# The context's modulation columns: from row products on DVE to float32 matmuls, started four steps sooner

## The chip, the core and the metric

One core of a Trainium2 chip runs the whole program in a single launch. The metric is the device time of one execution in microseconds (us). The kernel before took 3189.59 us, the median of three runs (3187.55 to 3194.36).

## The reference, cut to what matters

The program is a two-layer block (attention and a large product-key expert layer) on 256 tokens of width 1024, followed by a second block with recurrent mixers and a mixture of experts. The second block starts its recurrent states from a context of 256 rows. The context is normalised and modulated, and the modulation is what the change touches:

```
def _modulation(cvec, w, b, n):
    m = jax.nn.silu(cvec) @ w[:, : n * D_MODEL] + b[: n * D_MODEL]
    return jnp.split(m, n, axis=-1)
...
cm = _modulation(c_ctx, w_mod[i], b_mod[i], 2 if last else 6)
hc = _rmsnorm(ctx, norm_mix_pre[i]) * (1.0 + cm[1]) + cm[0]
sf_c = _state_features(hc, w_in[i], gdn_conv[i], gdn_a_log[i], gdn_dt_bias[i])
```

There is one layer here, so `n` is 2. A vector of 1024 values goes through SiLU and is multiplied by a 1024 x 2048 float32 weight, 8 MB. None of it depends on the first block's tokens. It can be worked out at any time before the context's features are needed.

## The kernel before, in words

Activations stand transposed: features on the 128 partitions, tokens along the free dimension. A weight tile is 128 x 1024 float32, 512 KB, loaded by a DMA from SP's queue. For the large projections `slot` splits it into a rounded high part on ACT (L281) and a remainder on DVE or POOL (L285), and each product takes three matmuls of these halves (`mm3`). The first four remainders of a phase go to POOL.

The opening runs two strands at once. The main strand is the first block: `ln_in` loads x, normalises it and transposes it on TensorE into h; `attention` projects keys, queries and values, rotates keys and queries (`rope`), splits them (`qsplit`, `ksplit`) and goes on to the scores. The side strand is the generator `context1` (L1234): the modulation, the context's normalisation, its features (`gdn_feat`) and its retention states. `tick(n)` runs the side strand n steps further, where a step is the work up to the next `yield`. So the places of the `tick` calls, with the numbers in `STEPS`, set the program order of the two strands. The scheduler that fills each engine's queue goes by a priority that follows the program order, with side instructions set back by `lag`, 100 places in the first layer, and by when it expects an instruction's inputs and buffers to be ready. Each engine then works through its queue in order.

The side strand has 20 steps. In the kernel before, two run at the end of `ln_in`, three after the key's split, four after the first query pair's rotation, four after the second's, three after the value projection, then two after each of two further query pairs.

The modulation in the kernel before: the vector c_ctx is loaded as one row broadcast to 128 partitions (`silu_row`, L947) and passed through SiLU. The weight lies with output columns on the partitions, so one tile of 128 outputs x 1024 inputs gives 128 modulation values: DVE multiplies the tile by the row and sums along the free dimension (L1247). Sixteen tiles make the 16 columns of `mctx`. The tiles take turns in the side strand's staging buffers rawB, whiB and wloB, two of each, which the context's projections use later. The first step only allocates; eight steps do two tiles each; the next two do the context's normalisation and transposes.

PSUM is handed out by `ps`: main work takes psA, side work psB, two buffers each.

Of the kernel before, what the change touches and what calls it, by code (L numbers as in the profile page):

```python
# [17 lines left out]
AF = mybir.ActivationFunctionType  # L18
OP = mybir.AluOpType
# [3 lines left out]
P = 128  # L23
D = 1024
S = 256
NT = 2
NC = 8
L = 2
# [102 lines left out]
def _colspec():  # L131
    s = [("lnin_g", 8), ("lnin_b", 8)]
    for l in range(L):
        s += [(f"ln1_g{l}", 8), (f"ln1_b{l}", 8), (f"ln2_g{l}", 8), (f"ln2_b{l}", 8), (f"gn{l}", 8), (f"qn{l}", 1), (f"kn{l}", 1)]
    s += [("mixpre", 8), ("ffnpre", 8), ("mixpost", 8), ("ffnpost", 8), ("bmod", 48), ("conv", 36), ("retgn", 4), ("gdnw", 4)]
    return s


# [4 lines left out]
def _pack(a):  # L143
    f = np.float32
    A = {k: np.asarray(v) for k, v in a.items()}
    out = _consts()
    col = lambda v: np.ascontiguousarray(v.reshape(-1, P).T)
    dup = lambda v: np.concatenate([v, v])[:, None]
    cols = {"lnin_g": col(A["ln_in_g"]), "lnin_b": col(A["ln_in_b"])}
    for l in range(L):  # L150
        cols[f"ln1_g{l}"], cols[f"ln1_b{l}"] = col(A["ln1_g"][l]), col(A["ln1_b"][l])
        cols[f"ln2_g{l}"], cols[f"ln2_b{l}"] = col(A["ln2_g"][l]), col(A["ln2_b"][l])
        cols[f"gn{l}"] = col(np.concatenate([A["gn_a_g"][l], A["gn_b_g"][l]]))
        cols[f"qn{l}"], cols[f"kn{l}"] = dup(A["qn_g"][l]), dup(A["kn_g"][l])
    cols["mixpre"], cols["ffnpre"] = col(A["norm_mix_pre_2"][0]), col(A["norm_ffn_pre_2"][0])
    cols["mixpost"], cols["ffnpost"] = col(A["norm_mix_post_2"][0]), col(A["norm_ffn_post_2"][0])
    cols["bmod"] = col(A["b_mod_2"][0])
    cv = A["gdn_conv_2"][0]
    cols["conv"] = np.concatenate([col(cv[k]) for k in range(3)], 1)
    cols["retgn"], cols["gdnw"] = col(A["ret_gn_w_2"][0]), col(A["gdn_norm_w_2"][0])  # L160
    out["cols"] = np.ascontiguousarray(np.concatenate([cols[n] for n, _ in COLSPEC], 1))
    rows = {"sink0": A["sink"][0], "sink1": A["sink"][1], "rdecay": A["ret_log_decay_2"][0].reshape(-1),
            "alog": A["gdn_a_log_2"][0].reshape(-1), "dtb": A["gdn_dt_bias_2"][0].reshape(-1), "rbias": A["router_bias_2"][0]}
    out["rows"] = np.ascontiguousarray(np.concatenate([rows[n] for n, _ in ROWSPEC])[None])
    out["brows"] = np.ascontiguousarray(np.stack([A["ln2_g"][L - 1], A["ln2_b"][L - 1], A["c_2"][0], A["c_ctx_2"]]))

    def tslots(w):
        k, n = w.shape
        return np.ascontiguousarray(w.reshape(k // P, P, n // P, P).transpose(2, 1, 0, 3)).reshape(n // P, P, -1)

    def kslots(w):
        k, n = w.shape
        return np.ascontiguousarray(w.reshape(k // 512, 4, P, n // 256, 256).transpose(3, 0, 2, 1, 4)).reshape(n // 256, k // 512, P, -1)

    hd = lambda b, h: np.arange(b + h * 64, b + h * 64 + 64)
    perm = [np.arange(512, 640), np.arange(1280, 1408)]
    perm += [np.concatenate([hd(0, t), hd(0, t + 4)]) for t in range(4)]
    perm += [np.concatenate([hd(768, t), hd(768, t + 4)]) for t in range(4)]
    perm = np.concatenate(perm)
    permv = np.concatenate([np.arange(640, 768), np.arange(1408, 1536)])  # L180
    out["win"] = np.stack([tslots(A["w_in"][l][:, perm]) for l in range(L)])
    out["winv"] = np.stack([kslots(A["w_in"][l][:, permv])[0] for l in range(L)])
    out["wo"] = np.stack([kslots(A["w_o"][l]) for l in range(L)])
    out["wq"] = np.stack([tslots(A["peer_wq"][l]) for l in range(L)])
    out["keys"] = np.ascontiguousarray(A["peer_keys"].transpose(0, 4, 1, 2, 3)).reshape(L, P, 2, 1024)
    u = A["peer_u"].reshape(L, 128, 128, 8, 128)
    out["u"] = np.ascontiguousarray(u.transpose(0, 2, 4, 3, 1)).reshape(L, 128, P, 1024)
    out["v"] = A["peer_v"].reshape(L, 128, 128, 1024)
    out["x"] = A["x"][0]
    out["ctx"] = A["ctx_2"][0]  # L190
    out["wmod"] = np.ascontiguousarray(A["w_mod_2"][0].T).reshape(48, P, D)
    w = A["w_in_2"][0]
    out["wrkv"] = kslots(w[:, 0:1024])
    out["wt2"] = tslots(np.concatenate([w[:, 0:512], w[:, 1024:2048], w[:, 2064:]], 1))
    out["wgab"] = np.ascontiguousarray(w[:, 2048:2064].reshape(NC, P, 16).transpose(1, 0, 2)).reshape(P, -1)
    t4 = lambda m: np.ascontiguousarray(m.reshape(4, P, 4, 2, P).transpose(2, 1, 3, 0, 4)).reshape(4, P, -1)
    out["wro"] = t4(A["w_ret_out_2"][0])
    out["wgo"] = t4(A["w_gdn_out_2"][0])
    out["wo2"] = kslots(A["w_o_2"][0])
    out["wr"] = np.ascontiguousarray(A["w_router_2"][0].reshape(NC, P, NE).transpose(1, 0, 2)).reshape(P, -1)  # L200
    gu = lambda g, u: np.concatenate([g, u], -1).reshape(-1, 4, 2, P, 512).transpose(0, 1, 3, 2, 4).reshape(-1, 4, P, 1024)
    out["moegu"] = np.concatenate([gu(A["w_sh_gate_2"][None], A["w_sh_up_2"][None]), gu(A["w_gate_2"][0], A["w_up_2"][0])])
    out["moed"] = np.concatenate([A["w_sh_down_2"].reshape(1, 2, P, 1024), A["w_down_2"][0].reshape(NE, 2, P, 1024)])
    return {k: np.ascontiguousarray(v, f) for k, v in out.items()}
# [4 lines left out]

STEPS = ((3, 4, 3, 2, 0, 1), (2, 1, 3, 2, 0, 3))
GSTEPS = (1, 0, 1, 2, 0, 1, 1, 0, 2, 0, 2, 1, 1, 1, 0, 0, 0, 2, 0, 0, 0, 0, 0, 2)


class K:
# [262 lines left out]
    def ln_in(self, a):  # L479
        nc = self.nc  # L480
        with self.tc.tile_pool(name="lnin", bufs=1) as pool:
            ys = []
            for t in range(2):
                ys.append(self.t(pool, [D], "lny", bufs=2))
                nc.sync.dma_start(ys[t], self.I["x"][t * P:(t + 1) * P, :])
            self.load_consts()
            for t, y in enumerate(ys):
                z = self.normalize(pool, [y[:, 0:512], y[:, 512:]], t)
                self.to_T(z, a, self.col["lnin_g"], self.col["lnin_b"], t)
            self.tick(2)  # L490
# [47 lines left out]
    def attention(self, l, a):  # L538
        nc, I = self.nc, self.I
        with ExitStack() as es:  # L540
# [61 lines left out]
            self.ksplit(KK[:, 0], KL[:, 0], ksb)  # L602
            self.tick(STEPS[l][0])
            qrope(0, qg0)
            self.tick(STEPS[l][1])
            qsum(1, sq1)
# [627 lines left out]
    def context1(self, es):  # L1234

        nc, I, tc = self.nc, self.I, self.tc
        cp = es.enter_context(tc.tile_pool(name="c1", bufs=1, side="right"))
        a = self.act(cp, NC, "hc", False)
        yield
        with tc.tile_pool(name="cm", bufs=1, side="right") as mp:  # L1240
            cb = self.t(mp, [D], "cb")
            self.silu_row(cb, 3)
            for j in range(16):
                pr = self.t(self.st, [D], ("rawB", "whiB", "wloB")[j % 3], bufs=2)
                nc.sync.dma_start(pr, I["wmod"][j])
                eng = nc.vector
                eng.scalar_tensor_tensor(pr, pr, 1.0, cb, op0=OP.mult, op1=OP.mult, accum_out=self.mctx[:, j:j + 1])  # L1247
                if j % 2:
                    yield
            nc.vector.tensor_tensor(self.mctx, self.mctx, self.col["bmod"][:, 0:16], op=OP.add)  # L1250
            g = self.scale_col(mp, self.col["mixpre"], self.mctx[:, 8:16], "cg")
            for t in range(NT):
                y = self.t(mp, [D], "cty", bufs=2)
                nc.sync.dma_start(y, I["ctx"][t * P:(t + 1) * P, :])
                self.to_T(self.rms_z(mp, y), a, g, self.mctx[:, 0:8], t, mp)
                yield
        self.dbg("hcT", a.hi.bitcast(F32).rearrange("p a n -> p (a n)"))
        fp = es.enter_context(tc.tile_pool(name="c2", bufs=1, side="right"))
        cs = self.t(fp, [self.CS], "cs")
        yield from self.gdn_feat(self.feat_views(cs), a, fp)  # L1260
        nc.sync.dma_start(self.dfeat, cs)
        rS = self.t(fp, [2, 512], "rS")
        yield from self.ret_states(fp, a, rS)
        nc.sync.dma_start(self.dret, rS.rearrange("p d n -> p (d n)"))
# [732 lines left out]
```

## Time and profile before

| | us |
|---|---|
| median of three runs | 3189.59 |
| lowest and highest | 3187.55, 3194.36 |
| profiled execution, its own time | 3194.2 |
| span in the profile, first to last instruction | 3192.4 |
| PE busy | 3017.8 |
| DVE busy | 2460.4 |
| ACT busy | 1636.2 |

PE is TensorE, PEld its weight loads, DVE VectorE, ACT ScalarE, POOL GpSimd, SP the engine that issues most DMAs. A line such as L1247 is one of the kernel file; names such as whiB are tiles, with buffer numbers left out. The granted clock is the share of full speed that TensorE's throttle gave; matmul ends are modelled, so PE can look busy while it is not at its peak.

### The profile page before, as it was taken

Reading aid. Unit: us, or ns where it says so; the run is one execution under the profiler, and the core shown is the slowest. Engines: PE = TensorE matmul, PEld = TensorE weight load, DVE = VectorE, ACT = ScalarE, POOL = GpSimd, SP = SyncE. Lnnn points to the kernel's source line nnn. Section 1 sums busy time; section 2 is a strip of 40 time slices with the busy share of each in tenths; the row PEclk is TensorE's granted clock in tenths of the full one; section 3 lists DMA queues with packets and bytes.
Section 4 is the critical chain, followed back from the end, with each engine's and each line's share of the span. In section 5 each row is a group of like instructions: output and inputs, shape, how many; then the busy total and the mean of one; then the engine's idle time right before and its main releaser. Section 6 shows DMA issues by size and latency. Waiting matters only on the chain. (4 is left out here: it accounts for less than half of the span.)

```text
span 3192.4 us, 51605 instructions
## 1 busy us (share of the span) xinstructions
PE 3017.8 (95%) x19882; PEld 2710.4 (85%) x19882; DVE 2460.4 (77%) x4140; ACT 1636.2 (51%) x2298; POOL 517.0 (16%) x311
## 2 busy tenths in 40 slices
PE   5999999999999799999999999978998999999997
PEld 5889999998888688999999888878997787777776
DVE  7555998876677776699887767767777888888886
ACT  4554444454544434444445454443344677766675
POOL 2010220000000423122000000012323222222221
PEclk8899999999999899999999999989998999999999
DMA  6335555567788312555556778842232887787875
GB/s 250 104 103 172 172 177 199 194 216 245 235 264 277 123 40 80 179 179 175 199 196 221 249 229 275 264 154 73 93 126 97 286 304 278 285 288 277 293 281 187
DMA packets 181199, 641.80 MB, mean 201 GB/s; under 512 B 20816, under 2 KB 21328, under 8 KB 180304
## 3 DMA queue, kind: packets, MB, share of 16 engines
q1 hardware_dynamic: 175824, 621.64, 57.0%
q0 software_dynamic: 5120, 16.78, 1.3%
q8 instruction: 158, 2.59, 0.3%
q14 instruction: 97, 0.79, 0.1%
HBM read 617.87 MB, written 20.46 MB: 200 GB/s over the span
## 5 line engine op out<-in xcount | busy, mean ns | idle before, releaser
L281 ACT CAST whiB<-rawB 128x1024 fp32r<-128x1024 f32 x433 | 454.1, 1049 | 446.0 <-PE psB L254 171.8
L281 ACT CAST whiA<-rawA 128x1024 fp32r<-128x1024 f32 x423 | 443.5, 1049 | 406.6 <-PE psA L254 159.4
L285 DVE TENSOR_TENSOR wloA<-rawA,whiA 128x1024 fp32r<-128x1024 f32 x390 | 515.1, 1321 | 154.9 <-ACT whiA L281 148.3
L285 DVE TENSOR_TENSOR wloB<-rawB,whiB 128x1024 fp32r<-128x1024 f32 x405 | 507.2, 1252 | 126.7 <-ACT whiB L281 121.9
L285 POOL TENSOR_TENSOR xlo<-xraw,xhi 128x1024 fp32r<-128x1024 f32 x64 | 170.1, 2658 | 520.6 <-ACT xhi L281 510.5
L254 PE MATMUL psA<-hh,whiA 128*128 128x256 f32 x840 | 244.7, 291 | 6.2 <-ACT hh L294 5.7
L254 PE MATMUL psA<-hh,wloA 128*128 128x256 f32 x840 | 243.4, 290 | 7.5 <-POOL wloA L285 6.5
L254 PE MATMUL psA<-hl,whiA 128*128 128x256 f32 x840 | 243.2, 290 | 2.9 <-DVE hl L295 2.9
L254 PE MATMUL psB<-hh,wloB 128*128 128x256 f32 x832 | 238.4, 287 | 4.8 <-DVE wloB L285 4.8
L254 PE MATMUL psB<-hh,whiB 128*128 128x256 f32 x832 | 239.6, 288 | 0.1
L254 PE MATMUL psB<-hl,whiB 128*128 128x256 f32 x832 | 237.7, 286 | 0.0
L254 PE MATMUL acc<-whiA,hh 128*128 128x512 f32 x512 | 199.2, 389 | 0.0
L254 PE MATMUL acc<-wloA,hh 128*128 128x512 f32 x512 | 199.2, 389 | 0.0
L254 PE MATMUL acc<-whiB,hh 128*128 128x512 f32 x512 | 199.2, 389 | 0.0
L254 PE MATMUL acc<-wloB,hh 128*128 128x512 f32 x512 | 199.2, 389 | 0.0
L254 PE MATMUL acc<-whiA,hl 128*128 128x512 f32 x512 | 199.2, 389 | 0.0
L254 PE MATMUL acc<-whiB,hl 128*128 128x512 f32 x512 | 199.2, 389 | 0.0
L285 POOL TENSOR_TENSOR wloB<-rawB,whiB 128x1024 fp32r<-128x1024 f32 x28 | 74.5, 2662 | 739.7 <-ACT whiB L281 739.7
L285 POOL TENSOR_TENSOR wloA<-rawA,whiA 128x1024 fp32r<-128x1024 f32 x33 | 87.3, 2650 | 628.1 <-DVE zlnry L363 348.2
L254 PEld LDWEIGHTS psA<-hh,wloA 128*128 128x128 f32 x840 | 165.3, 197 | 9.0 <-POOL wloA L285 7.3
L254 PEld LDWEIGHTS psA<-hh,whiA 128*128 128x128 f32 x840 | 165.1, 197 | 7.2 <-ACT hh L294 6.5
L254 PEld LDWEIGHTS psA<-hl,whiA 128*128 128x128 f32 x840 | 165.0, 196 | 3.9 <-POOL wloA L285 1.9
(842 smaller groups left out, 8660.6 us busy)
## 6 DMA issues: line engine op xcount, KB each, us to landing
rawA<-in_moegu SPq DMA_DIRECT2D x130, 512.0 KB, 4.7
rawB<-in_moegu SPq DMA_DIRECT2D x130, 512.0 KB, 5.2
rawA<-in_u SPq DMA_DIRECT2D x128, 512.0 KB, 3.4
rawB<-in_u SPq DMA_DIRECT2D x128, 512.0 KB, 3.3
rawA<-in_v SPq DMA_DIRECT2D x128, 512.0 KB, 4.5
rawB<-in_v SPq DMA_DIRECT2D x128, 512.0 KB, 4.5
xraw<-in_moed SPq DMA_DIRECT2D x128, 512.0 KB, 5.9
rawB<-in_wt SPq DMA_DIRECT2D x40, 512.0 KB, 3.2
```

The costliest lines, as they stand in the source:

```text
L254: self.pe = self.nc.tensor.matmul(out, lhsT, rhs, start=start, stop=stop, skip_group_check=True).ins
L281: self.nc.scalar.copy(hi[:, :n], w[:, :n])
L285: i = (eng or self.nc.vector).tensor_tensor(lo[:, :n], w[:, :n], hi[:, :n].bitcast(F32), op=OP.subtract)
```

## The change

The weight of the two modulation vectors is laid out a second time as `wmodc`, with inputs on the partitions, in the tile form of the other projections. The vector c_ctx becomes eight columns of the constants tile (`cctx`) and leaves the rows that are broadcast. A SiLU runs over 128 x 8 values. For each of eight steps n, two tiles are loaded; each tile is eight 128 x 128 weights that stand in the array while one column of the vector moves through, accumulating over the eight input chunks into one PSUM column. DVE adds the bias while it reads the two columns out of PSUM. Arithmetic is plain float32.

A `tick(4)` is put into `ln_in` ahead of the normalisation, and `STEPS` for the first layer is lowered by one at its first three entries, of which the second is used twice.

```diff
-    s += [("mixpre", 8), ("ffnpre", 8), ("mixpost", 8), ("ffnpost", 8), ("bmod", 48), ("conv", 36), ("retgn", 4), ("gdnw", 4)]
+    s += [("mixpre", 8), ("ffnpre", 8), ("mixpost", 8), ("ffnpost", 8), ("bmod", 48), ("cctx", 8), ("conv", 36), ("retgn", 4), ("gdnw", 4)]
...
+    cols["cctx"] = col(A["c_ctx_2"])
...
+    out["wmodc"] = tslots(A["w_mod_2"][0][:, 0:2 * D])
...
-STEPS = ((3, 4, 3, 2, 0, 1), (2, 1, 3, 2, 0, 3))
+STEPS = ((2, 3, 2, 2, 0, 1), (2, 1, 3, 2, 0, 3))
...
             self.load_consts()
+            self.tick(4)
             for t, y in enumerate(ys):
...
-            cb = self.t(mp, [D], "cb")
-            self.silu_row(cb, 3)
-            for j in range(16):
-                pr = self.t(self.st, [D], ("rawB", "whiB", "wloB")[j % 3], bufs=2)
-                nc.sync.dma_start(pr, I["wmod"][j])
-                eng = nc.vector
-                eng.scalar_tensor_tensor(pr, pr, 1.0, cb, op0=OP.mult, op1=OP.mult, accum_out=self.mctx[:, j:j + 1])
-                if j % 2:
-                    yield
-            nc.vector.tensor_tensor(self.mctx, self.mctx, self.col["bmod"][:, 0:16], op=OP.add)
+            cc = self.t(mp, [8], "cc")
+            nc.scalar.activation(cc, self.col["cctx"], AF.Silu)
+            for n in range(8):
+                ps = self.ps()
+                for z in range(2):
+                    w = self.t(self.st, [D], ("rawB", "whiB", "wloB")[(2 * n + z) % 3], bufs=2)
+                    nc.sync.dma_start(w, I["wmodc"][2 * n + z])
+                    for c in range(NC):
+                        self.mm(ps[:, z:z + 1], w[:, c * P:(c + 1) * P], cc[:, c:c + 1], z + c == 0, z == 1 and c == NC - 1)
+                nc.vector.tensor_tensor(self.mctx[:, 2 * n:2 * n + 2], ps[:, 0:2], self.col["bmod"][:, 2 * n:2 * n + 2], op=OP.add)
+                yield
```

## Rows read from the trace of the kernel before

**Rows 1.** The page, part 1: PE's busy time, share of span, instructions.

```profile
PE 3017.8 (95%) x19882; PEld 2710.4 (85%) x19882; DVE 2460.4 (77%) x4140; ACT 1636.2 (51%) x2298; POOL 517.0 (16%) x311
```

**Rows 2.** Opening by stretch: length, busy time by engine, granted clock, DMA share, GB/s.

```profile
0.00:22.00 22.00, 4.61 (x17) 3.29 (x17) 13.06 (x43) 11.82 (x18) 7.09 (x10) 1.00 0.79 274
22.00:49.00 27.00, 23.77 (x156) 22.74 (x155) 20.80 (x38) 7.31 (x12) 11.09 (x8) 0.94 0.83 311
49.00:64.40 15.40, 5.77 (x24) 2.84 (x23) 13.41 (x35) 9.28 (x20) 3.71 (x3) 0.73 0.38 154
64.40:100.00 35.60, 33.27 (x249) 32.62 (x250) 27.54 (x61) 23.58 (x37) 0.00 (x0) 0.88 0.56 179
100.00:140.00 40.00, 32.28 (x209) 28.61 (x208) 20.78 (x45) 19.56 (x37) 0.00 (x0) 0.79 0.24 80
140.00:230.00 90.00, 89.69 (x699) 81.74 (x698) 53.89 (x157) 43.44 (x101) 7.60 (x5) 1.00 0.27 94
```

**Rows 3.** Timeline of PE: start, us, instruction, [idle before <-releaser].

```profile
21.59 0.58 PE L254 MATMUL psA<-hh,whiA 128*128 128x256 f32 x1 [2.00 <-ACT hh L294]
...
64.39 0.58 PE L254 MATMUL psA<-whiA,hh 128*128 128x256 f32 x1 [8.13 <-ACT whiA L281]
67.08 1.97 PE L262 MATMUL psB<-cst,rmsz 128*128 128x128 f32 x8 [2.10 <-DVE rmsz L970]
...
106.09 0.55 PE L254 MATMUL psA<-KK,Q 128*128 128x256 f32 x1 [2.18 <-DVE Q L527]
...
133.60 1.97 PE L262 MATMUL psB<-cst,gvT 128*128 128x128 f32 x8 [4.68 <-ACT gvT L994]
```

**Rows 4.** Line 1247's row products: count, min/median/max ns, first and last start.

```profile
L1247 DVE SCALAR_TENSOR_TENSOR rawB<-rawB,cb x6: 1219/1225/1411, 16.1 to 62.2; 128x1024 f32<-128x1024 f32 x6
L1247 DVE DVE_READ_ACCUMULATOR rawB<-rawB,cb x6: 77/81/83, 17.4 to 63.3; 128x1 f32 x6
L1247 DVE SCALAR_TENSOR_TENSOR whiB<-whiB,cb x5: 1209/1221/3309, 18.7 to 50.5; 128x1024 f32<-128x1024 f32 x5
...
L1247 DVE SCALAR_TENSOR_TENSOR wloB<-wloB,cb x5: 1211/1218/1226, 21.1 to 52.0; 128x1024 f32<-128x1024 f32 x5
```

**Rows 5.** Timeline of ACT, POOL and DVE near the start.

```profile
10.64 1.03 ACT L281 CAST whiA<-rawA 128x1024 fp32r<-128x1024 f32 x1
...
11.75 4.65 POOL L285 TENSOR_TENSOR wloA<-rawA,whiA 128x1024 fp32r<-128x1024 f32 x2 [11.32 <-ACT whiA L281]
...
14.99 1.06 ACT L950 ACTIVATE cb<-cb 128x1024 f32<-128x1024 f32 x1
...
16.07 1.41 DVE L1247 SCALAR_TENSOR_TENSOR rawB<-rawB,cb 128x1024 f32<-128x1024 f32 x1 [1.96 <-ACT cb L950]
```

**Rows 6.** Timeline of SP's queue.

```profile
3.06 0.91 SPq L266 DMA_DIRECT2D rawA<-in_win  x2
```

**Rows 7.** DMA issues of the opening: size of one, median us to landing.

```profile
rawA<-in_win SPq DMA_DIRECT2D x6, 512.0 KB, 3.8
...
cb<-in_brows SPq DMA_DIRECT2D x1, 512.0 KB, 8.6
```

**Rows 8.** Timeline of PE: float32 matmuls in a row, merged.

```profile
100.36 1.91 PE L254 MATMUL psB<-cst,ssq 128*128 128x1 f32 x16
...
109.03 3.78 PE L254 MATMUL psB<-cst,zgkry 128*128 128x128 f32 x16 [0.86 <-DVE zgkry L363]
```

**Rows 9.** Two shorter stretches, columns as in rows 2.

```profile
64.40:73.00 8.60, 6.50 (x29) 6.21 (x30) 8.60 (x26) 4.80 (x8) 0.00 (x0) 0.50 0.75 237
...
106.00:114.00 8.00, 7.05 (x27) 6.00 (x28) 4.33 (x10) 3.58 (x9) 0.00 (x0) 0.50 0.31 112
```

**Rows 10.** Timelines of ACT and DVE ahead of the value projection.

```profile
56.27 1.66 ACT L535 CAST KK<-ksb 64x256 fp32r<-64x256 f32 x4 [4.79 <-DVE ksb L505]
...
63.30 1.99 ACT L281 CAST whiA<-rawA 128x1024 fp32r<-128x1024 f32 x2
63.47 0.16 DVE L1250 TENSOR_TENSOR mctx<-mctx,cols 128x16 f32<-128x16 f32 x1
```

More of the change, by code (lines that the diff above doesn't have):

```diff
@@ L164, in _pack @@
     out["rows"] = np.ascontiguousarray(np.concatenate([rows[n] for n, _ in ROWSPEC])[None])
-    out["brows"] = np.ascontiguousarray(np.stack([A["ln2_g"][L - 1], A["ln2_b"][L - 1], A["c_2"][0], A["c_ctx_2"]]))
+    out["brows"] = np.ascontiguousarray(np.stack([A["ln2_g"][L - 1], A["ln2_b"][L - 1], A["c_2"][0]]))
     def tslots(w):
```

## The prediction

> **What bounds the kernel now.** The page's first part comes first: TensorE is busy for 3017.8 of 3192.4 us [rows 1]. Most of the program is a stream of matmuls with almost no gaps, so only gaps, or matmuls at the half clock, can be won. The change touches the context's side work alone, so I next cut the opening into stretches [rows 2]. From 140 us on PE is busy for 89.69 of 90 us. Before that it isn't: 4.61 of the first 22 us, 23.77 of the 27 us from 22 to 49, 5.77 of the 15.4 us from 49 to 64.4, 33.27 of 35.6 and 32.28 of 40 us after it. In those stretches the granted clock is 0.94, 0.73, 0.88 and 0.79, a mix of the full 2.4 GHz and half of it. Whatever this change is worth is decided between 10 and 140 us; later work starts sooner or later by the same amount.
>
> What ends PE's waits there? At the start the normalised input: the first projection matmul starts at 21.59, after ACT and DVE have turned h into its two halves. Then one wait of 8.13 us before the V projection at 64.39, for ACT's cast whiA; 2.10 us for the context's rmsz; 2.18 us for a Q half; 4.68 us for the context's gvT [rows 3]. The two engines named were not free for the main path: DVE is busy for 20.80 of the 27 us and 13.41 of the 15.4 us [rows 2], and the row products of the changed lines are the large optional share of that.
>
> **What goes.** Sixteen row products on DVE: medians 1.225, 1.221 and 1.218 us, and one of 3.31, beside a POOL subtraction; each is followed by an accumulator read of 0.08 [rows 4]. With their means that is 6 x 1.267 + 5 x 1.637 + 5 x 1.220 = 21.9 us, and 16 x 0.08 = 1.3: 23.2 us of DVE. The SiLU over 1024 columns (1.06 us on ACT) goes, and so does its 512 KB broadcast load, which took 8.6 us to land [rows 5, 7]. An 8-column SiLU takes their place. Its ACT table load stays, likely earlier; its cost has the old 1.06 us as upper end and zero as the lower. I take zero, as the work is a hundredth.
>
> **What comes.** 128 float32 matmuls of one column. The nearest row is the same form: 16 float32 matmuls of 128x1 in 1.91 us, 0.119 each. At the half clock the nearest row is 16 float32 matmuls, 128x128, in 3.78 us, 0.236 each, in a stretch whose granted clock is 0.50 [rows 8, 9]. So 128 cost 15.2 us at the full clock (taken, since PE now has work between the projections) and 30.2 us at the other end; below 15 nothing excludes a little, as single ends are modelled. Eight small additions on DVE replace one of 0.16 us [rows 10] (between the main path's operations, 1.1 us more); one addition ends each group and frees its PSUM buffer, two of which alternate. The queue of PE is in order: behind a modulation matmul that waits for its 512 KB tile stand the transposes of h and the projections, and ACT and DVE wait for those.
>
> **What moves.** Four steps are put ahead of the normalisation. The first only opens; the next three issue six weight tiles on SP, 48 matmuls and three additions. Now the first two win tiles go out on SP at 3.06 us [rows 6], and every modulation tile later. In program order the six tiles now come early; a side step's priority is set back by 100 places, and by my count of the instructions between them they still precede win. So the main loads pass behind 6 x 512 KB. At the 311 GB/s of the stretch from 22 to 49 [rows 2] one tile takes 1.69 us, six 10.1. Four later places take one step fewer each, until the counts meet at the V projection (16 steps before and after), so nothing after that is moved in program order, and the queues of POOL and ACT get the same work behind it.
>
> **The sum, stretch by stretch** (against the profiled execution: span 3192.4, its own time 3194.2, while the three timed runs have a median of 3189.59).
>
> 1. To the first projection. ACT loses 1.06 us and DVE two row products (1.41 and, by the median, 1.22) that stand between hr and hl now [rows 4, 5], so h is ready about 3.7 us sooner if nothing else were late. Next late is the weight: win lands near 3.06 + 3.8 [rows 6, 7] + 10.1 = 17 us, its cast takes 1.03 and POOL's subtraction 4.65 for two [rows 5]: about 20.3 for the first, 22.7 for the second, where the second is needed one tile of matmuls later. That leaves 1.5 of the 3.7 us: **-1.5** (ends -3.7 and +1, the latter if the transposes stand behind six tiles that land one per 1.69 us).
> 2. 22 to 49. By 22 us the DMA engines moved 22 x 274 GB/s = 6.0 MB, at a busy share of 0.79; with cb gone and the holes filled that is room for about eight modulation tiles beside x, constants and win. The other eight, 64 matmuls, add 64 x 0.119 = 7.6 us to PE. The stretch has 27 - 23.77 = 3.2 us free, and 0.06 x 27 = 1.6 us is what its lower clock costs at most. **+3** (ends: -4.8, all tiles before 22 and both losses gone; +12, all sixteen in it with only the 3.2 us filled).
> 3. 49 to 64.4. Three row products (two here at 1.3 with their reads, and one at 62.20) leave DVE's chain: 3.9 us. The key's rotation, which now queues with the queries' because its small steps wait between row products, can move ahead of it, about 3 us more by my reading. The cover that remains is ACT's order: KK at 56.27, the Q casts, the rmsz squares, whiB, and only then whiA at 63.30 [rows 10]. **-6** (ends: 0, if whiA still comes last after the same work; -8.1, the whole wait).
> 4. After 64.4. The modulation ends near 49 instead of 63.5, so the context's rmsz wait of 2.10 us is gone or filled: **-2** (ends 0 and -9, if the waits of 2.18 and 4.68 go too).
>
> -1.5 + 3 - 6 - 2 = **-6.5 us**: 3187.7 in the profiled execution's terms, **3183.1** beside the median of the timed runs.
>
> Weighing the clock: the rows say that PE stands at the half clock after its longest wait, 0.50 from 64.4 to 73 us, while its matmuls follow each other [rows 9]. The Trainium skill, in "TensorE: Matmul & The Clock Gate", section "HAM oscillation — how this bites in real kernels", states that bursts of matmuls shorter than the wait for the next DMA keep the clock throttled; read so, it speaks against this change and is the third rival below; the trace of before has no such bursts to show it.
>
> **Rivals.**
> - *Larger gain.* The context's features come so early that PE's later waits (2.18 and 4.68, and some half-clock time in 100 to 140) are filled as well: -6.5 - 7.5 = -14, **3176**. For it: the granted clock of 0.79 there [rows 2] shows how much lies open. Against: those waits are chains within the features, whoever starts first.
> - *The wait stays.* whiA still stands last in ACT's order, the side work fills that time as before, and PE has only the added matmuls: -1.5 + 3 = +1.5, **3191**. For it: side and main work stands ahead of whiA in that order now [rows 10].
> - *Half clock.* A tile's eight matmuls take 0.95 us, its transfer 1.69, so PE works in short bursts and the 64 matmuls after 22 us cost 0.236: 64 x 0.117 = 7.5 more: +1, **3190.5**. Against: between bursts there are projections.
> - *Slower: PE becomes the bound.* Most modulation matmuls fall into 22 to 49, where PE is 88% busy. Fifteen or sixteen tiles there cost 15.2 - 3.2 = +12; with -6 and -1.5 from steps 3 and 1, and step 4 paid by a later start (+2), that is +6.5 to +7, **3196.5**. It decides once what comes after 22 us exceeds 3.2 + 1.5 + 6 = 10.7 us, 90 matmuls or 11 tiles. For it: main loads wait behind six tiles. Against: PE has 17 free us before 22.
>
> **Chances.** Forecast 0.50 (own range 3178 to 3188), larger gain 0.15, wait stays 0.13, half clock 0.07, slower 0.15. A difference of 0.2% (6.4 us) is about what measurement tells from none. Half of the forecast's chance is beyond it, all of the larger gain, and 0.02 of the spread of the next two: faster 0.42. Same: 0.25 of the forecast, 0.14 of these two, 0.02 of the last: 0.41. Slower: 0.13 and 0.04 of their upper ends: 0.17. Range: from 3173, below the larger gain, to 3198, just over the slower case, leaves out the tails of both, and the joint ends of the four steps (-25.6 and +13).
>
> **What would show it.** Right: no row product on DVE; groups of float32 128x1 matmuls on PE from about 10 us, near 0.12 us each; the last addition of the columns before 52 us; the V projection's first matmul near 60 instead of 64.39; and PE's stream at 140 us some 6 us ahead. Step 1 is wrong if the first projection matmul starts after 23 us with PE waiting for a modulation tile or for win; step 2 if the sixth weight tile of the projections ends much after 50; step 3 if a wait of 8 us before V is still there. The forecast falls as a whole if the lead at 64 us is lost by 140 us to waits inside the context's features.

## The result and the profile after

The changed kernel takes a median of 3230.65 us (3222.45 to 3233.53), the kernel before 3190.62 us beside it: a ratio of 1.0119, interval 1.0105 to 1.0132. It is 40 us slower. The forecast was 3183.1, the range ended at 3198.

The page of the changed kernel, its span and the first line of part 1, which answers to [rows 1]:

```profile
span 3230.4 us, 52091 instructions
PE 3069.6 (95%) x20138; PEld 2764.5 (86%) x20138; DVE 2444.3 (76%) x4115; ACT 1634.8 (51%) x2297; POOL 511.2 (16%) x311
```

Against the profiled execution of before (span 3192.4) the span grew by 38.0 us. TensorE's busy time grew by 51.8 us (3069.6 - 3017.8), its idle time fell by 13.8 us (174.6 to 160.8). So TensorE didn't come to wait more; it came to work longer. And it has 256 more instructions (20138 - 19882), where 128 matmuls were added: each float32 matmul leaves two records (a record is one entry of the profile).

The opening of the changed kernel by stretch, in the columns of [rows 2] (length, busy time of PE, PEld, DVE, ACT, POOL, granted clock, DMA share, GB/s):

```profile
0.00:22.00 22.00, 11.20 (x54) 11.23 (x54) 8.67 (x36) 5.94 (x10) 0.19 (x4) 1.00 0.57 211
22.00:49.00 27.00, 27.00 (x155) 27.00 (x156) 4.18 (x12) 9.05 (x16) 12.22 (x13) 0.93 0.66 237
49.00:64.40 15.40, 15.40 (x81) 15.40 (x82) 3.22 (x12) 2.12 (x3) 2.18 (x1) 0.57 0.64 239
64.40:100.00 35.60, 30.34 (x165) 27.82 (x163) 13.63 (x41) 10.14 (x21) 3.56 (x3) 0.61 0.16 58
100.00:140.00 40.00, 36.64 (x261) 35.74 (x261) 26.29 (x52) 24.54 (x38) 0.00 (x0) 0.83 0.49 160
```

DVE is relieved: over the run it is busy for 16.1 us less (2460.4 - 2444.3). In the second stretch it falls from 20.80 to 4.18 us and in the third from 13.41 to 3.22, which is more, as the main work that it serves comes later too (from 100 to 140 us it is busy for 26.29 us, 20.78 before). TensorE has taken over. From 22 to 64.4 us it is busy without a gap (42.40 of 42.40), yet in the third stretch it runs at a granted clock of 0.57, and at 0.61 in the one after. A TensorE that is never idle and still at half clock for most of the time is the row to stop at.

The timeline of TensorE in the changed kernel (start, us, instruction, idle before in brackets) shows the added matmuls as groups of x16, one for each weight tile:

```profile
10.80 3.55 PE L256 MATMUL psB<-cc,rawB 128*128 128x1 f32 x16 [10.80 <-DMA rawB<-in_wmodc]
14.21 1.95 PE L264 MATMUL psA<-cst,lnz 128*128 128x128 f32 x8
15.95 3.41 PE L256 MATMUL psB<-cc,whiB 128*128 128x1 f32 x16
...
34.48 0.56 PE L256 MATMUL psA<-hh,whiA 128*128 128x256 f32 x1
...
82.50 1.93 PE L256 MATMUL psB<-cc,whiB 128*128 128x1 f32 x16
84.28 1.93 PE L256 MATMUL psB<-cc,wloB 128*128 128x1 f32 x16
...
91.33 3.41 PE L256 MATMUL psB<-cc,rawB 128*128 128x1 f32 x16
...
100.66 0.58 PE L256 MATMUL psA<-whiA,hh 128*128 128x256 f32 x1 [5.91 <-ACT whiA L283]
```

A tile's 8 matmuls are 16 records. They take 3.41 to 3.55 us (3.41 is 0.213 each) in most places, and 1.93 us (0.121) where projections had just gone ahead of them. Two short stretches of the same kernel give the clock at two such places, and TensorE is busy throughout in both:

```profile
69.98:73.40 3.42, 3.42 (x18) 3.42 (x18) 0.00 (x0) 0.00 (x0) 0.00 (x0) 0.50 0.00 0
...
82.50:86.00 3.50, 3.50 (x33) 3.50 (x31) 1.57 (x4) 1.74 (x5) 0.73 (x1) 0.98 0.00 0
```

The first stretches need care. Up to 38.2 us the granted clock reads 1.00, but TensorE's own matmuls say otherwise:

```profile
10.80:38.20 27.40, 27.40 (x129) 27.40 (x130) 5.97 (x15) 8.05 (x15) 9.65 (x11) 1.00 0.56 202
```

```profile
37.61 0.41 PE L256 MATMUL psA<-hh,wloA 128*128 128x256 f32 x1
37.82 0.41 PE L256 MATMUL psA<-hh,whiA 128*128 128x256 f32 x1
...
38.39 0.28 PE L256 MATMUL psA<-hh,whiA 128*128 128x256 f32 x1
38.51 0.28 PE L256 MATMUL psA<-hl,whiA 128*128 128x256 f32 x1
```

The same projection matmuls follow one another every 0.21 us before that point and every 0.12 us after it, and the five one-column tiles from 15.95 on take 3.41 to 3.55 us each, as in the stretch at 0.50. So TensorE ran at half pace, without a gap, from 10.80 to 38.2 us. The trace's first entry for the clock lies there; ahead of it the column shows 1.00, which is too high, and so is the 0.93 of the second stretch.

All modulation matmuls of the changed kernel together, cut out by the tile of the vector (same columns, engines without a row left off):

```profile
0.00:110.00 110.00, 47.94 (x256) 50.97 (x256) 0.21 (x1) 0.75 0.48 172
```

That is 47.94 us of TensorE. The first projection starts at 34.48 (21.59 before, [rows 3]), the V projection at 100.66 (64.39): 36.3 us late. Ahead of V TensorE was busy for 34.1 and idle for 30.3 us before [rows 2]; now it is busy for 83.9 and idle for 16.7. The lateness is carried almost unchanged to the end: the first matrix load of the next stage is issued at 312.7 in place of 276.2 (36.5 late), that of the expert stage at 2427.2 in place of 2390.4 (36.8). Everything is decided before V.

### The profile page after: what moved, and what is told of

The parts are those of the page before. It is cut to its first block, busy times and chain, and to the rows that moved or that the text cites. A ratio compares the mean times of both kernels' runs of the same rounds, so it can differ in the third digit from the quotient of the medians.

```text
span 3230.4 us, 52091 instructions
## 1 busy us (share of the span) xinstructions
PE 3069.6 (95%) x20138; PEld 2764.5 (86%) x20138; DVE 2444.3 (76%) x4115; ACT 1634.8 (51%) x2297; POOL 511.2 (16%) x311
```

## The experiments

Three things came together in the change: float32 matmuls of one column, their count, and the early start. The first batch takes them apart.

**Matmuls without the early start.** From the kernel after:

```diff
-STEPS = ((2, 3, 2, 2, 0, 1), (2, 1, 3, 2, 0, 3))
+STEPS = ((3, 4, 3, 2, 0, 1), (2, 1, 3, 2, 0, 3))
...
-            self.tick(4)
```

> The float32 matmuls without the early start (no steps ahead of the normalisation, step counts of before). Theory passes (each float32 matmul is two records on PE, 256 in all, 48 us of PE work in the changed kernel, on the engine that bounds the opening): still 25 to 45 us slower than before, 3213 to 3233. Rival order (the loss comes from six weight tiles and 96 records put ahead of the transposes of h and of the win loads): within 6 us of before, 3185 to 3197.

Measured: 3228.91 us, ratio to before 1.0119 (1.0102 to 1.0136), beside 3230.65 with the early start. The place is not the cause. Two rows of this kernel's TensorE:

```profile
22.53 0.58 PE L256 MATMUL psA<-hh,whiA 128*128 128x256 f32 x1 [1.05 <-ACT hh L296]
...
103.17 0.58 PE L256 MATMUL psA<-whiA,hh 128*128 128x256 f32 x1 [5.82 <-ACT whiA L283]
```

The first projection is nearly back in its place, V is even later: the same work (48.75 us of modulation records) only lies behind the first projection instead of ahead of it.

**The early start alone**, with the row products left on DVE. From the kernel before:

```diff
-STEPS = ((3, 4, 3, 2, 0, 1), (2, 1, 3, 2, 0, 3))
+STEPS = ((2, 3, 2, 2, 0, 1), (2, 1, 3, 2, 0, 3))
...
+            self.tick(4)
```

> The row products on DVE with the early start. Theory passes: no slower than before, 3180 to 3194, as nothing is added to PE. Rival order: the first projection matmul moves from 21.6 to about 30 us and the time rises by 10 to 30 us, 3200 to 3220.

Measured: 3198.60, ratio 1.0024 (1.0014 to 1.0034): 7 us slower, between the two expectations and in neither. The early tiles cost a little by themselves. TensorE of this kernel:

```profile
24.33 0.58 PE L254 MATMUL psA<-hh,whiA 128*128 128x256 f32 x1 [3.50 <-ACT hh L294]
...
67.21 0.58 PE L254 MATMUL psA<-whiA,hh 128*128 128x256 f32 x1 [9.32 <-DVE zrqy L349]
```

The first projection is 2.7 us later than in [rows 3], V 2.8 us later and now behind DVE's chain. Of the 40 us at most 7 belong to the start; the matmuls carry the rest.

**Half of the matmuls.** From the kernel after, with every second input chunk of the modulation left out:

```diff
-                    for c in range(NC):
+                    for c in range(0, NC, 2):
-                        self.mm(ps[:, z:z + 1], w[:, c * P:(c + 1) * P], cc[:, c:c + 1], z + c == 0, z == 1 and c == NC - 1)
+                        self.mm(ps[:, z:z + 1], w[:, c * P:(c + 1) * P], cc[:, c:c + 1], z + c == 0, z == 1 and c == NC - 2)
```

> The changed kernel with every second input chunk of the modulation left out: 64 matmuls, all 16 tiles still loaded. Theory passes: half of the 48 us of PE time goes and comes off the end, 20 to 27 us faster than the changed kernel, 3203 to 3211. Rival order: 3225 to 3232, as loads and places stay.

Measured: 3207.64, ratio 1.0049 (1.0029 to 1.0068): 23.0 us less than after. The modulation matmuls of this kernel, as cut out above, and its V projection:

```profile
0.00:110.00 110.00, 22.68 (x128) 24.22 (x128) 0.21 (x1) 0.84 0.56 197
```

```profile
79.81 0.58 PE L256 MATMUL psA<-whiA,hh 128*128 128x256 f32 x1 [8.12 <-ACT whiA L283]
```

25.3 us of records went (47.94 - 22.68), 20.9 us of it shows at V and 23.0 at the end. The time of these matmuls lies on the path, nearly microsecond for microsecond. It is still open whether that time comes from their count or from the clock.

**The same matmuls at the full clock** (the wide kernel below). From the kernel after: DVE copies the vector so that each column stands 128 times, and each matmul moves 128 equal columns, of which one is read. Count, weights and order stay.

```diff
+            cw = self.t(mp, [8, P], "cw")
+            nc.vector.tensor_copy(cw, cc.unsqueeze(2).broadcast_to([P, 8, P]))
...
-                        self.mm(ps[:, z:z + 1], w[:, c * P:(c + 1) * P], cc[:, c:c + 1], z + c == 0, z == 1 and c == NC - 1)
+                        self.mm(ps[:, z * P:(z + 1) * P], w[:, c * P:(c + 1) * P], cw[:, c, :], z + c == 0, z == 1 and c == NC - 1)
-                nc.vector.tensor_tensor(self.mctx[:, 2 * n:2 * n + 2], ps[:, 0:2], self.col["bmod"][:, 2 * n:2 * n + 2], op=OP.add)
+                nc.vector.tensor_tensor(self.mctx[:, 2 * n:2 * n + 2], ps[:, 0:2 * P].rearrange("p (z n) -> p z n", z=2)[:, :, 0], self.col["bmod"][:, 2 * n:2 * n + 2], op=OP.add)
```

> The changed kernel with the vector's column repeated 128 times as moving operand, so each modulation matmul gives 128 equal columns, of which one is read. Theory clock (one-column matmuls leave TensorE at the half clock, so a record takes 0.21 us and not the 0.12 seen at the full clock, and the projections among them run slow too): the clock rises within the first tiles, a record falls to 0.12 to 0.14 us, time 3205 to 3218. Rival: a record costs its weight load whatever the columns, and the clock stays: 3229 to 3236.

Measured: 3194.26 (ten runs), ratio 1.0011 (0.9997 to 1.0024): 36.4 us less than after, for 128 times the columns. That is below the 3205 to 3218 that was expected: the theory had the sign right and the size too small. Stretches of this kernel:

```profile
22.00:49.00 27.00, 26.67 (x229) 26.47 (x228) 5.72 (x17) 8.03 (x13) 10.55 (x6) 1.00 0.89 330
49.00:64.40 15.40, 14.87 (x121) 13.49 (x120) 13.46 (x36) 8.65 (x18) 3.71 (x3) 1.00 0.42 137
64.40:100.00 35.60, 31.96 (x260) 30.91 (x260) 29.18 (x57) 24.63 (x39) 0.00 (x0) 0.98 0.46 151
```

Its modulation matmuls, cut out as above:

```profile
0.00:110.00 110.00, 34.77 (x256) 32.87 (x256) 0.69 (x1) 0.00 (x0) 0.97 0.61 216
```

And TensorE's timeline:

```profile
20.77 1.95 PE L256 MATMUL psB<-cw,whiB 128*128 128x128 f32 x16
22.56 1.95 PE L256 MATMUL psB<-cw,wloB 128*128 128x128 f32 x16
24.27 0.36 PE L256 MATMUL psA<-hh,whiA 128*128 128x256 f32 x1
...
66.25 0.36 PE L256 MATMUL psA<-whiA,hh 128*128 128x256 f32 x1
```

Up to 64.4 us TensorE is no busier than in the changed kernel (14.87 against 15.40 of 15.40 us in the third stretch), but the granted clock is 1.00, 1.00 and 0.98 in place of 0.93, 0.57 and 0.61. One tile follows another after 1.79 us (20.77 to 22.56), in place of 3.3 to 3.4. The first projection starts 10 us sooner than after, V 34.4 us sooner.

**The copy with one column.** The last kernel differs from the changed one by the copy as well. So, from the wide kernel, with the copy kept:

```diff
-                        self.mm(ps[:, z * P:(z + 1) * P], w[:, c * P:(c + 1) * P], cw[:, c, :], z + c == 0, z == 1 and c == NC - 1)
+                        self.mm(ps[:, z * P:z * P + 1], w[:, c * P:(c + 1) * P], cw[:, c, 0:1], z + c == 0, z == 1 and c == NC - 1)
```

> The wide kernel with the same 128-fold copy of the vector on DVE, but each matmul reads and writes one column of it. Theory clock: back to the half clock and to a record of 0.21 us, 3222 to 3234. Rival (the copy's place and the order it brings made the wide kernel fast): 3191 to 3200.

Measured: 3230.59, ratio 1.0121 (1.0098 to 1.0144), the time of the kernel after. The third and fourth stretch of this kernel, and V:

```profile
49.00:64.40 15.40, 15.40 (x80) 15.40 (x80) 3.25 (x12) 2.15 (x3) 1.74 (x1) 0.56 0.65 239
64.40:100.00 35.60, 29.93 (x165) 27.54 (x163) 14.01 (x41) 10.51 (x21) 3.57 (x3) 0.62 0.17 58
```

```profile
100.26 0.58 PE L256 MATMUL psA<-whiA,hh 128*128 128x256 f32 x1 [5.93 <-ACT whiA L283]
```

Two kernels that differ only in how many columns each matmul reads and writes lie 36 us apart, at 0.56 and 1.00 of the clock in the third stretch. So the matmuls of one column bring the half clock. Their mean granted clocks over the run, 0.971 and 0.979, make 0.029 x 3227.5 - 0.021 x 3194.5 = 26.5 us, beside 33.0 us between the two profiled spans. This is an estimate only: it leaves out the half pace ahead of the first entry for the clock (up to about 38 us in the one-column kernel, 13 in the wide one), and it counts idle time too. By it the half clock is most of the slowdown.

**Wide and without the early start**: the wide kernel with the first experiment's edit.

```diff
-STEPS = ((2, 3, 2, 2, 0, 1), (2, 1, 3, 2, 0, 3))
+STEPS = ((3, 4, 3, 2, 0, 1), (2, 1, 3, 2, 0, 3))
...
-            self.tick(4)
```

> 128 equal columns and no early start, the fourth corner of two by two. Theory clock: the drop from the late one-column kernel (3229) is as large as with the early start, 30 to 38 us, so 3190 to 3198, and order is worth less than 6 us either way. Rival (the wide kernel was fast because its instructions stand in another order): 3205 to 3230 here, as this order is that of the late kernel.

Measured: 3196.41, ratio 1.0015 (1.0002 to 1.0028). With it the table is complete (medians, us; before 3191.43 and 3192.06 beside them):

| | late start | early start |
|---|---|---|
| row products on DVE | 3191 to 3192 (before) | 3198.60 |
| float32, one column | 3228.91 | 3230.65 (after) |
| float32, 128 columns | 3196.41 | 3194.26 |

With matmuls the order is worth 2 us either way, which these runs don't tell from nothing; the columns are worth 32.5 us (late) and 36.4 us (early).

**Wide, and half of the matmuls** (the half-wide kernel below): the wide kernel with the third experiment's edit.

```diff
-                    for c in range(NC):
+                    for c in range(0, NC, 2):
```

> The wide kernel with every second input chunk left out, 64 matmuls of 128 columns. Theory: at the full clock the modulation still takes 256 x 0.111 = 28 us of PE, of which half goes here; if PE bounds the opening throughout, 10 to 14 us faster than the wide kernel, 3180 to 3185; if the matmuls only fill waits now, within 4 us of it, 3190 to 3197.

Measured: 3194.66, ratio 1.0016 (1.0001 to 1.0030), the same as wide with all of them. At half clock halving the matmuls gave 23 us, at the full clock it gives nothing that shows. Yet V is sooner, as the TensorE rows of this kernel show:

```profile
58.86 0.39 PE L256 MATMUL psA<-whiA,hh 128*128 128x256 f32 x1 [1.64 <-ACT whiA L283]
...
62.99 1.94 PE L264 MATMUL psB<-cst,rmsz 128*128 128x128 f32 x8 [3.75 <-DVE zrmst L358]
...
67.22 0.58 PE L256 MATMUL psA<-wloA,hh 128*128 128x256 f32 x1 [2.28 <-DVE wloA L287]
...
109.07 0.35 PE L256 MATMUL psA<-KK,Q 128*128 128x256 f32 x1 [3.80 <-DVE Q L530]
...
131.87 1.54 PE L264 MATMUL psB<-cst,gvT 128*128 128x128 f32 x6 [2.72 <-ACT gvT L997]
```

V is 5.5 us ahead of [rows 3], the matmul behind gvT only 1.7 us (131.87 against 133.60), the next stage's first load 1.3 us (274.9 against 276.2). Most of the lead at V is lost to waits of both strands: 3.75 us for the context's normalisation (2.10 for the matmul of the same name in [rows 3]), 2.28 us for the V projection's split weights, and 3.80 us for Q (2.18 in [rows 3]).

## Why the prediction was wrong

**The step that failed is the second, by the price of one matmul.** The prediction took "128 cost 15.2 us at the full clock" and, out of them, 64 in the stretch from 22 to 49. They cost 47.94 us, 38.34 of them after 22 us. The step's own sign came: the sixth weight tile of the projections was not to end much after 50 us, and its last matmul starts at 81.44 (48.73 before). The term was mis-sized twice:

- *The count.* The row "x16 in 1.91 us" of [rows 8] was read as 16 matmuls; it is 16 records of 8 matmuls. The second line there, which looked like 16 matmuls as well, misled in the same way. 256 records at 0.119 are 30.5 us: 15.2 more than forecast. The page of before could not say so by itself, but a count would have: the number of float32 matmuls that the source issues in one such place against the x of its group.
- *The clock.* 47.94 - 30.5 = 17.5 us more. The mean granted clock of the whole run, 0.975 before and 0.970 after, can't confirm this size, because it misses the half pace ahead of 38.2 us.

Of the 51.8 us more of TensorE the modulation is 47.9: the 15.2 that were forecast, and 32.7 of these two errors. Of the two it is the clock that decides the time: with every record at full clock the wide kernel takes 3194.26 us, and with half of them 3194.66. The worst end that the prediction gave for all 128, "30.2 us at the other end", is about the cost at the full clock.

The step also took the clock of its stretch from the column, "0.06 x 27 = 1.6 us is what its lower clock costs at most". The kernel before starts at half pace too, up to about 28.7 us:

```profile
28.37 0.41 PE L254 MATMUL psA<-hl,whiA 128*128 128x256 f32 x1
...
28.79 0.28 PE L254 MATMUL psA<-hh,whiA 128*128 128x256 f32 x1
28.91 0.28 PE L254 MATMUL psA<-hl,whiA 128*128 128x256 f32 x1
```

So 1.6 us was no upper end.

**The half clock was seen and dismissed for the wrong reason.** The rival priced it at 7.5 us, "bursts" between waits for DMA, and set "between bursts there are projections" against it. There were no waits: after the first 10.8 us TensorE doesn't wait for a transfer in the opening at all, it is busy for 15.40 of 15.40 us at 0.57. The Trainium skill, in "TensorE: Matmul & The Clock Gate", section "What's actually happening", lets the clock follow how busy the engine has lately been; read by the profile's busy time, that would have put this stretch at full speed. The trace does not agree, and the measurement decides: with float32 matmuls of one column in it the stretch stood at 0.57. The section that the prediction weighed, "HAM oscillation — how this bites in real kernels" in the Trainium skill, pointed the right way, but its waits for a DMA are not what happened here.

**"Slower: PE becomes the bound" was the right rival with too small a price.** It decides, the prediction says, once the matmuls after 22 us exceed 10.7 us. They do, with 38.34 us. Its price was +6.5 to +7 us, because it took 15.2 us where 47.94 stood. The sign was right.

**Step 1** (-1.5) was overrun. Half of its sign of failure came, a first projection after 23 us (34.48); the other half did not, since TensorE was not waiting for a tile or for win but busy with the modulation. The loads are late as well. SP's queue in the changed kernel:

```profile
3.34 0.43 SPq L1250 DMA_DIRECT2D rawB<-in_wmodc  x1
...
24.65 0.33 SPq L400 DMA_DIRECT2D csta<-in_csta  x1
25.50 0.91 SPq L268 DMA_DIRECT2D rawA<-in_win  x2
```

The win tiles go out at 25.50, where the prediction had win landed near 17 us. They stand in SP's queue behind csta, and csta's load waits for the transposes of h (psA, L264), which stand in TensorE's queue among the modulation's matmuls. SP's waits show it (us in total, times, longest):

```profile
SPq L400 <- PE psA L264: 13.9, 1, 13.9
```

At full clock the delay shrinks: the wide kernel starts its first projection at 24.27.

**Step 3** (-6) held as a mechanism where TensorE left room. V stands at 58.86 in the half-wide kernel, with 18.91 us of modulation records, close to the 15.2 us that the prediction counted on; "near 60" was forecast. In the kernel after, TensorE's own work hides that gain, though the wait ahead of V did fall, from 8.13 to 5.91.

**Step 4** (-2) falls, and with it the forecast, much as the prediction's own last condition says: in the half-wide kernel most of the lead at V is lost by 140 us to waits, of the context's features and of the main strand. So the half-wide kernel, with modulation work near what was forecast, shows no gain of 6.5 us; the wide kernels stand 2 to 5 us above before, at the edge of what can be told apart. In the changed kernel the sign for this step came late too, the last addition of the columns (the timeline of DVE):

```profile
96.27 0.15 DVE L1253 TENSOR_TENSOR mctx<-psB,cols 128x2 f32<-128x2 f32 x1
```

It was forecast before 52 us.

**Open.** The wide kernel is ahead by 4.9 us at the first load of the next stage (271.3 against 276.2) and not at the end. In its profiled execution the expert stage took 808.0 us, 802.0 before; across the kernels it lies between 801.5 and 808. Whether that is chance from one execution to the next or follows from the change was not settled. Nor was it tried to let the weights stream past the vector, in place of the vector past the weights.

## What to carry to other kernels

Before work goes from another engine to TensorE, find out what one of its instructions costs in this very form, and count the records that one call leaves: here one float32 matmul is two. A matrix-vector product in one-column matmuls held TensorE at half clock here although it never idled, and the work that shared the stretch ran at it too; look at the granted clock beside the busy time, not at the busy time alone. If such a product must stand there, columns that are thrown away may be cheaper than a single one. Here even that only came back to the time of the kernel before, whose product stood on DVE.

## What was not expected of the hardware

- TensorE busy for all of 15.40 us at a granted clock of 0.57, and for all of 3.42 us at 0.50, with float32 matmuls of one column in its work; 1.00 in the third stretch with 128 columns and the same weights. 128 columns cost no more per record (16 in 1.95 us) than one column at full clock (16 in 1.93 us).
- The granted clock reads 1.00 ahead of its first entry in the trace, while matmuls that take 0.12 us later follow every 0.21 us (27.4 us of it in the changed kernel).
- The clock reaches the neighbours as well. Between the kernel after and the wide one TensorE's busy time differs by 34.0 us (3069.6 against 3035.6 on the wide kernel's page), of which the modulation's records are 13.2 (47.94 against 34.77). The other 20.8 us, worked out as the remainder, lie in the matmuls around them. Most of it is a gain over the kernel before and no loss of the changed one: without the modulation TensorE is busy for 3017.8 us before, 3021.7 after and 3000.8 in the wide kernel. So the wide matmuls win back about half of their own 34.77 us in the work around them.
- One of these float32 matmuls is two records on TensorE: 20138 - 19882 = 256 for 128.
